# One hybrid decoder layer: another queue for the modulation rows, a later place for two kinds of stores

## The chip, the cores and the metric

The kernel runs on one core of a Trainium2 chip. The metric is the device time of one execution in microseconds (us). The engines are TensorE (PE), VectorE (DVE), ScalarE (ACT), GpSimd (POOL) and SyncE (SP). Each works through its own instructions in order. A transfer between HBM and the core's memory is issued by one of these engines as an instruction of its own; in the kernel before nearly all are issued by SP.

## What is computed

One layer for a sequence of 2048 tokens of width 1024, in float32:

```python
mod = jax.nn.silu(c) @ w_ada + b_ada                       # 6 * 1024 modulation values
shift1, scale1, gate1, shift2, scale2, gate2 = split(mod, 6)
h = rmsnorm(x, norm1_w) * (1 + scale1) + shift1
proj = h @ w_in                                            # q, k, v, z, xbc, dt
attn = sliding_window_attention(rope(q), rope(k), v, sinks)  # window 128
xbc = silu(causal_depthwise_conv(xbc, conv_w, conv_b))     # 1024 channels, width 4
y = ssd_chunked_scan(...) * silu(z), normalised by group   # Mamba-2, 8 heads, state 128
x = x + gate1 * (concat(attn, y) @ w_out)
h = rmsnorm(x, norm2_w) * (1 + scale2) + shift2
x = x + gate2 * ((silu(h @ w_g) * (h @ w_u)) @ w_down)     # width 2816
return rmsnorm(x, final_norm_w)
```

## The kernel before

Tokens are worked on in four blocks of 512. Every matrix product is made of three passes over halves: an operand is split into a high part (a rounded copy, made by ACT) and a low part (the difference, made by DVE or POOL), and `mm3` multiplies high by high, high by low and low by high.

**Weights.** `weight` (L259) makes one weight tile. The first block to use it loads the raw weight (L266, tile `raw`, 5 buffers), splits it (ACT L267, POOL or DVE L268, tile `w`, 6 buffers) and stores the two halves to HBM (L271); later blocks load the halves (L263). The stores are 16 of `wx` in block 0's `convolved`, 8 of `wz` in block 0's `gated`, 8 of `wq` and 4 of `wkv` in block 1, and 16 of `wo` in block 0's `out_proj`. That is 52 stores, of 512 KB (`wkv` 528 KB) each.

**Conv.** `convolved` (L467) makes the 8 tiles of 128 channels of a block with two weights each, runs the width-4 convolution over ACT, DVE and POOL, and stores each result tile `sx` (2 buffers) to `xs` in HBM (L490), 32 stores in all. The SSD part reads `xs` back by L682 in chunks of 128 tokens.

**Modulation.** The opening makes shift1 and scale1. The 32 other columns that are needed (gate1, scale2, shift2, gate2) are made by `ada_later` (L183), one column of 128 values per call: two loads of 256 KB each (L188, tile `aw`, 2 buffers), and a reduction on DVE for each (L194). The second reduction adds to the first. `tc.issue_after(last_fetched.ins)` ahead of the loads ties those that are issued by the engine of `last_fetched`, which is SP, to a place behind that instruction; the reductions are tied behind `first_done` on DVE in the same way. `rest_of_ada` calls `ada_later` for all 32 columns. It is attached to the main loop in block 2, but its loads start at 42.5 us.

**Order.** PE's order is that of the text (`manual_schedule`). In the opening the order of DVE, SP and ACT is that of the text too, among the instructions of the opening. Everywhere else a planner sets the order of each engine: it plays the program through with estimated times and issues, on each engine, what is ready, the earlier in the text first. The main loop goes through queries, keys and values, conv and gate of each block; `tick` (L1257) runs pieces of attention, SSD and other side work between the weights. Norms ahead of a block load x twice (L332), make the squares (L281, L284), and then the operands `hl` (DVE L324, ACT L326, DVE L327).

After the mixing part come the feed-forward products (`quad` and `down`, L949 and following), which the change does not touch.

Of the kernel before, what the change touches and what calls it, by code (L numbers as in the profile page):

```python
# [11 lines left out]
F32 = mybir.dt.float32  # L12
# [30 lines left out]
def hymba_layer(ctx, tc, xT, crow, pos, wada, wadk, vecs, rows, wq, wkv, wz, wx, wo, wgu, wd4, wd2, outT):  # L43
    nc = tc.nc
# [10 lines left out]
    def big(tag, bufs, dt=F32, pool=sb):  # L55
        return pool.tile([P, T], dt, name=tag, tag=tag, bufs=bufs)
# [8 lines left out]
    def dense():  # L65
        return bank("d", 4)
# [30 lines left out]
    def small(shape, name, bufs=2, dt=F32, pool=sb):  # L97
        return pool.tile(shape, dt, name=name, tag=name, bufs=bufs)
# [84 lines left out]
    def ada_later(i):  # L183
        halves = [slice(0, T), slice(T, D)]
        ws = [big("aw", 2, pool=ip) for _ in halves]
        with tc.issue_after(last_fetched.ins):
            for w, hs in zip(ws, halves):
                nc.sync.dma_start(w, wada[i, :, hs])  # L188
        for _ in range(2):
            yield  # L190
        m, pt = mod[:, i:i + 1], small([P, 1], "part", 2, pool=ip)
        with tc.issue_after(first_done.ins):
            for w, hs, src, dst in zip(ws, halves, (b_ada[:, i:i + 1], pt), (pt, m)):
                nc.vector.tensor_tensor_reduce(w, w, csil[:, hs], 0.5, src, ALU.mult, ALU.add, dst)  # L194
        yield
# [60 lines left out]

    split_d = {}

    def weight(src, n, key, store, eng=nc.gpsimd):  # L259
        two = wt.tile([P, 2, 528], F32R, name="w", tag="w", bufs=SPLIT)  # L260
        hi, lo = two[:, 0, :n], two[:, 1, :n]
        if key in split_d:
            nc.sync.dma_start(two[:, :, :n].bitcast(F32), split_d[key])  # L263
            return hi, lo
        raw = wt.tile([P, 528], F32, name="raw", tag="raw", bufs=RAW)
        nc.sync.dma_start(raw[:, :n], src)  # L266
        nc.scalar.activation(hi, raw[:, :n], AF.Copy)  # L267
        eng.tensor_tensor(lo, raw[:, :n], hi.bitcast(F32), ALU.subtract)  # L268
        if store:
            split_d[key] = dr.tile([P, 2, n], F32, name="w_" + "_".join(str(k) for k in key))  # L270
            nc.sync.dma_start(split_d[key], two[:, :, :n].bitcast(F32))  # L271
        return hi, lo

    def mm3(out, ahi, alo, bhi, blo, first, last):
        nc.tensor.matmul(out, ahi, bhi, start=first, stop=False)  # L275
        nc.tensor.matmul(out, ahi, blo, start=False, stop=False)  # L276
        mm3.last = nc.tensor.matmul(out, alo, bhi, start=False, stop=last)  # L277
# [85 lines left out]
    xs_d = [dr.tile([8, P, T], F32, name=f"xs{b}") for b in range(NB)]  # L363
# [18 lines left out]
    def tokens(b, h, name, srcs, n, toks, bank_of=lambda i: dense()):  # L382
        per = 2 if n == 256 else 1
        banks = [bank_of(i) for i in range(len(toks) // per)]
        plan = [(i, t, banks[i // per][:, i % per * n:i % per * n + n]) for i, t in enumerate(toks)]
        for kp in range(KT // 2):
            whi, wlo = weight(srcs[kp], 2 * n, (name, kp), b == (0 if name[0] == "z" else 1) and toks[-1] == NT - 1)
            for e in range(2):
                k, cs = 2 * kp + e, slice(e * n, (e + 1) * n)
                for i, t, out in plan:  # L390
                    ts = slice(t * P, (t + 1) * P)
                    mm3(out, h[k][0][:, ts], h[k][1][:, ts], whi[:, cs], wlo[:, cs],
                        k == 0 and i % per == 0, k == KT - 1 and i % per == per - 1)
            if kp < KT // 2 - 1 and (per == 2 or kp % 2):
                yield
        return [(t, out) for _, t, out in plan]
# [70 lines left out]
    def convolved(b, h):  # L467
        for c in range(8):
            ps = dense()
            for half in range(2):  # L470
                if half:
                    yield
                whi, wlo = weight(wx[c, half], T, ("x", c, half), b == 0, nc.gpsimd if half else nc.vector)
                for i in range(4):
                    k = 4 * half + i
                    ws = slice(i * P, (i + 1) * P)
                    mm3(ps, whi[:, ws], wlo[:, ws], h[k][0], h[k][1], k == 0, k == KT - 1)
            cin = small([P, T + 3], "cin", 2, pool=ip)
            nc.gpsimd.tensor_copy(cin[:, 0:3], halo[:, c, :])
            nc.scalar.copy(cin[:, 3:T + 3], ps)  # L480
            nc.gpsimd.tensor_copy(halo[:, c, :], cin[:, T:T + 3])
            cv, th, o = big("s", 3, pool=fw), big("s", 3, pool=fw), big("sx", 2, pool=ip)
            nc.scalar.activation(cv, cin[:, 0:T], AF.Identity, scale=conv_w[:, c, 0:1], bias=conv_b[:, c:c + 1])
            nc.scalar.activation(th, cin[:, 1:1 + T], AF.Copy, scale=conv_w[:, c, 1:2])
            nc.vector.scalar_tensor_tensor(cv, ps, conv_w[:, c, 3:4], cv, ALU.mult, ALU.add)
            nc.vector.scalar_tensor_tensor(th, cin[:, 2:2 + T], conv_w[:, c, 2:3], th, ALU.mult, ALU.add)
            nc.gpsimd.tensor_tensor(cv, cv, th, ALU.add)
            nc.scalar.activation(th, cv, AF.Tanh)
            nc.vector.scalar_tensor_tensor(o, th, 1.0, cv, ALU.add, ALU.mult)
            nc.sync.dma_start(xs_d[b][c], o)  # L490
            yield

    def gated(b, h):
        def gate(part, t, ps):
            z, th = staged(), big("s", 3, pool=fw)[:, 0:256]
            nc.scalar.activation(th, ps, AF.Tanh, scale=0.5)
            nc.vector.scalar_tensor_tensor(z, th, 1.0, ps, ALU.add, ALU.mult)
            nc.sync.dma_start(z_d[b * NT + t][:, part * 256:part * 256 + 256], z)
        yield from two_parts(b, h, "z", wz, gate)
# [746 lines left out]
    def rest_of_ada():  # L1246
        for i in (*range(16, 24), *range(32, 40), *range(24, 32), *range(40, 48)):
            yield from ada_later(i)
            if i == 39:
                nc.vector.scalar_tensor_tensor(scl2, mod[:, 32:40], 1.0, n2w, ALU.add, ALU.mult)  # L1250
            if i == 31:
                nc.vector.tensor_tensor(dsh, sh2[:, 4:8], sh2[:, 0:4], ALU.subtract)
        nc.vector.tensor_scalar(gate2, gate2, 0.5, None, ALU.mult)
# [56 lines left out]
    with tc.manual_schedule(engines={mybir.EngineType.PE}):  # L1310
# [8 lines left out]
        att = attentions(0, common)  # L1319
        sides.append(att)  # L1320
        run(convolved(0, h), 0.5)
        run(gated(0, h), 0.5)
        sides[:] = [both(att, ssds(0, stepping[0], extra))]
# [4 lines left out]
        run(keys_values(1, h), MIX)  # L1328
        prepared(1)
        run(convolved(1, h), MIX)  # L1330
        run(gated(1, h), MIX)
        mix1 = both(attentions(1, common), ssds(1, stepping[1], extra))
# [5 lines left out]
        prepared(2)  # L1338
        nxt = norm_ahead(3, (10, 15, 22))
        run(convolved(2, h), MIX)  # L1340
        finish(mix0)
        mix = []
# [163 lines left out]
def build(nc, arrays):  # L1506
    args = [nc.dram_tensor(f"in_{n}_dram", v.shape, mybir.dt.from_np(v.dtype), kind="ExternalInput").ap()
            for n, v in arrays.items()]
    out = nc.dram_tensor("out_0_dram", (NB, KT, P, T), F32, kind="ExternalOutput").ap()
    with tile.TileContext(nc, schedule_with_timeline_sim=True) as tc:  # L1510
        hymba_layer(tc, *args, out)
# [12 lines left out]
```

## Time and profile before

| | us |
|---|---|
| time, median of 3 runs | 2349.11 (2348.67 to 2351.01) |
| the profiled execution's own time | 2349.34 |
| its span, first to last instruction | 2347.3 |
| PE busy | 2239.9 |
| DVE busy | 1474.2 |
| POOL busy | 1216.1 |
| ACT busy | 969.8 |
| loads of modulation rows, first to last | 42.5 to 346.2 |
| stores of split weights, first to last | 70.0 to 546.1 |
| stores of conv results, first to last | 95.8 to 739.1 |

The span is 2.0 us shorter than the execution's own time. In the profile a row names line, engine, operation and the tiles written and read (`out<-in`); `SPq` and `ACTq` are the sequencers, which issue transfers and wait. A row of a wait names who waited, `<-` for whom, the total, how many times and the longest.

### The profile page before, as it was taken

To read this page: it belongs to the slowest core of one execution; us is meant where nothing else is said; L and a number is where in the kernel's file an instruction comes from. 1 tells how busy PE (TensorE), PEld (TensorE's weight loads), DVE (VectorE), ACT (ScalarE), POOL (GpSimd) and SP (SyncE) were. 2 spreads that over 40 slices of the span, in tenths; PEclk is the share of its full clock that TensorE was granted. 3 is DMA by queue.
4 is the path that set the end of the run, shared out by engine and by line. 5 is a ranking of instruction groups with operands and counts; after the bars stand their busy time and mean duration, and the time that the engine had idled before them with its cause. 6 is when DMAs were issued, how large, how long until landed. Compare 5 with 4: busy or idle time off the path is not lost. (4 is left out here: it accounts for less than half of the span.)

```text
span 2347.3 us, 33320 instructions
## 1 busy us (share of the span) xinstructions
PE 2239.9 (95%) x11292; PEld 1855.1 (79%) x11292; DVE 1474.2 (63%) x2629; ACT 969.8 (41%) x2020; POOL 1216.1 (52%) x1203
## 2 busy tenths in 40 slices
PE   6878989999999999999999999999999999999998
PEld 5778778888878788887877888767788888888787
DVE  8987975773578855666664353498645454454544
ACT  4564533654356645333333232344333333333332
POOL 2556433553223755687784332448666666653441
PEclk9989999999999999999999999999999999999999
DMA  8898887777888422332235765564422222273451
GB/s 299 296 322 305 301 252 251 252 245 254 291 271 310 141 72 81 101 99 88 95 102 164 256 217 177 185 222 144 144 81 81 81 81 81 81 227 102 142 172 63
DMA packets 252522, 418.52 MB, mean 178 GB/s; under 512 B 22848, under 2 KB 68928, under 8 KB 252352
## 3 DMA queue, kind: packets, MB, share of 16 engines
q1 hardware_dynamic: 251776, 415.87, 53.8%
q8 instruction: 89, 1.46, 0.3%
q14 instruction: 81, 0.66, 0.1%
q10 hardware_dynamic: 576, 0.52, 0.1%
HBM read 317.68 MB, written 98.63 MB: 177 GB/s over the span
## 5 line engine op out<-in xcount | busy, mean ns | idle before, releaser
L849 ACT ACTIVATE w<-raw 128x512 fp32r<-128x512 f32 x308 | 193.8, 630 | 428.5 <-PE d L277 225.1
L951 PE MATMUL d<-b,w 128*128 128x512 f32 x924 | 367.3, 399 | 1.3 <-POOL w L850 1.3
L949 PE MATMUL d<-b,w 128*128 128x512 f32 x924 | 365.1, 399 | 2.0 <-ACT t L980 1.3
L950 PE MATMUL d<-b,w 128*128 128x512 f32 x924 | 366.7, 397 | 0.3 <-POOL b L880 0.3
L275 PE MATMUL d<-a,w 128*128 128x512 f32 (+1 forms) x720 | 282.4, 396 | 10.2 <-DVE x L1060 5.2
L276 PE MATMUL d<-a,w 128*128 128x512 f32 (+1 forms) x720 | 282.2, 392 | 5.4 <-DVE a L844 5.3
L277 PE MATMUL d<-a,w 128*128 128x512 f32 (+1 forms) x720 | 283.9, 394 | 0.0
L850 DVE TENSOR_TENSOR w<-raw,w 128x512 fp32r<-128x512 f32 x220 | 209.0, 951 | 58.5 <-ACT w L849 57.7
L1060 DVE SCALAR_TENSOR_TENSOR x<-d,mod,x 128x512 f32<-128x512 f32 (+1 forms) x182 | 131.2, 724 | 173.9 <-PE d L277 171.9
L850 POOL TENSOR_TENSOR w<-raw,w 128x512 fp32r<-128x512 f32 x88 | 121.3, 1379 | 227.2 <-ACT w L849 209.9
L949 PEld LDWEIGHTS d<-b,w 128*128 128x128 f32 x924 | 174.3, 189 | 42.4 <-ACT t L980 2.5
L951 PEld LDWEIGHTS d<-b,w 128*128 128x128 f32 x924 | 174.0, 188 | 41.7 <-POOL w L850 1.5
L950 PEld LDWEIGHTS d<-b,w 128*128 128x128 f32 x924 | 174.6, 189 | 39.5 <-POOL b L880 0.7
L849 ACT ACTIVATE w<-s 128x512 fp32r<-128x512 f32 x176 | 111.1, 633 | 223.2 <-PE d L951 163.0
L850 POOL TENSOR_TENSOR w<-s,w 128x512 fp32r<-128x512 f32 x132 | 186.7, 1417 | 31.1 <-ACT w L849 30.3
L275 PE MATMUL d<-w,hl 128*128 128x256 f32 (+1 forms) x592 | 176.6, 298 | 7.7 <-ACT hl L326 5.0
L277 PE MATMUL d<-w,hl 128*128 128x256 f32 (+1 forms) x592 | 172.4, 291 | 2.2 <-DVE hl L327 2.2
L275 PEld LDWEIGHTS d<-a,w 128*128 128x128 f32 x720 | 136.3, 190 | 45.8 <-ACT a L1024 7.1
L276 PE MATMUL d<-w,hl 128*128 128x256 f32 (+1 forms) x592 | 172.1, 291 | 0.0
L276 PEld LDWEIGHTS d<-a,w 128*128 128x128 f32 x720 | 137.1, 190 | 38.3 <-DVE a L844 7.3
L277 PEld LDWEIGHTS d<-a,w 128*128 128x128 f32 x720 | 136.7, 190 | 30.4 <-issue 0.5
L965 POOL TENSOR_TENSOR s<-raw,s 128x512 f32<-128x512 f32 x44 | 58.6, 1332 | 186.7 <-DVE w L850 109.0
(393 smaller groups left out, 5437.7 us busy)
## 6 DMA issues: line engine op xcount, KB each, us to landing
raw<-in_wgu_dram SPq DMA_DIRECT2D x176, 256.0 KB, 2.7
raw<-in_wd_dram SPq DMA_DIRECT2D x176, 256.0 KB, 2.7
w<-w_x SPq DMA_DIRECT2D x48, 512.0 KB, 5.2
w<-w_o SPq DMA_DIRECT2D x48, 512.0 KB, 4.6
act<-t SPq DMA_DIRECT2D x88, 256.0 KB, 2.1
t<-act SPq DMA_DIRECT2D x88, 256.0 KB, 4.3
t<-in_xT_dram SPq DMA_DIRECT2D x80, 256.0 KB, 4.3
aw<-in_wada_dram SPq DMA_DIRECT2D x64, 256.0 KB, 4.5
```

Of the source, the lines that this page charges most:

```text
L275: nc.tensor.matmul(out, ahi, bhi, start=first, stop=False)
L276: nc.tensor.matmul(out, ahi, blo, start=False, stop=False)
L277: mm3.last = nc.tensor.matmul(out, alo, bhi, start=False, stop=last)
L849: nc.scalar.activation(hi, x, AF.Copy)
L850: eng.tensor_tensor(lo, x, hi.bitcast(F32), ALU.subtract)
L949: nc.tensor.matmul(out, ahi, bhi, start=first and k == 0, stop=False, skip_group_check=True)
L950: nc.tensor.matmul(out, ahi, blo, start=False, stop=False, skip_group_check=True)
L951: mm3.last = nc.tensor.matmul(out, alo, bhi, start=False, stop=k == 3, skip_group_check=True)
L965: nc.gpsimd.tensor_tensor(s4, a12, s2, ALU.subtract)
L1060: nc.vector.scalar_tensor_tensor(x, ps, gate2[:, c:c + 1], x, ALU.mult, ALU.add)
```

## The change

The loads in `ada_later` are issued by ACT in place of SP. The stores of split weights and of conv results are no longer issued where they stood: they are put on a list `owed` with a count of 2. Each call of `weight` first calls `settle`, which lowers the counts and issues on SP what has come to 0. At the end of `convolved` all that is still owed is issued. All bytes, tiles and buffer counts stay the same.

```diff
@@ ada_later
         with tc.issue_after(last_fetched.ins):
             for w, hs in zip(ws, halves):
-                nc.sync.dma_start(w, wada[i, :, hs])
+                nc.scalar.dma_start(w, wada[i, :, hs])
@@
+    owed = []
+
+    def settle():
+        for entry in list(owed):
+            entry[0] -= 1
+            if entry[0] == 0:
+                owed.remove(entry)
+                nc.sync.dma_start(*entry[1:])
+
     def weight(src, n, key, store, eng=nc.gpsimd):
+        settle()
...
-            nc.sync.dma_start(split_d[key], two[:, :, :n].bitcast(F32))
+            owed.append([2, split_d[key], two[:, :, :n].bitcast(F32)])
@@ convolved
-            nc.sync.dma_start(xs_d[b][c], o)
-            yield
+            owed.append([2, xs_d[b][c], o])
+            yield
+        for entry in list(owed):
+            owed.remove(entry)
+            nc.sync.dma_start(*entry[1:])
```

## The prediction

> **What bounds the kernel now.** I read the page first, then the busy times by stage, then who waits for whom in the stages that the change touches, then the queues' own order. The page says that TensorE (PE) is the bound almost everywhere.
>
> ```profile
> span 2347.3 us, 33320 instructions
> PE 2239.9 (95%) x11292; PEld 1855.1 (79%) x11292; DVE 1474.2 (63%) x2629; ACT 969.8 (41%) x2020; POOL 1216.1 (52%) x1203
> ```
>
> All of the idle time of PE is 2347.3 - 2239.9 = 107 us. The busy times by stage (columns: PE, its weight loads, DVE, ACT and POOL busy us with counts, then granted PE clock, DMA share, GB/s) show that the stretch from 60 to 352 us, where the modulation rows are loaded, holds 40 us of it, with a clock below 1 and DMA engines near full.
>
> ```profile
> 20.00:60.00 40.00, 39.79 (x266) 31.51 (x267) 37.51 (x57) 16.30 (x26) 12.31 (x9) 1.00 0.82 287
> 60.00:200.00 140.00, 116.89 (x685) 101.11 (x683) 118.24 (x277) 76.91 (x171) 69.53 (x68) 0.90 0.90 311
> 200.00:352.00 152.00, 134.72 (x876) 119.03 (x876) 128.76 (x321) 75.26 (x183) 78.69 (x117) 0.98 0.85 281
> ```
>
> That is (140.0 - 116.9) + (152.0 - 134.7) = 40.4 us, and it bounds from above what any mending of this stretch can give. DVE is busy for 85% of it, ACT for 52%. The waits of PE between 60 and 352 us (total, times, longest) say who ended the idle time.
>
> ```profile
> PE d L275 <- ACT hl L326: 5.0, 3, 2.3
> PE st L714 <- ACT m L793: 4.2, 1, 4.2
> PE am L275 <- ACT hl L326: 3.5, 1, 3.5
> PE at L589 <- DVE rsq L247: 3.3, 1, 3.3
> PE am L628 <- ACT m L592: 3.0, 1, 3.0
> PE d L277 <- DVE hl L327: 2.2, 4, 1.3
> PE d L275 <- ACT w L267: 2.1, 1, 2.1
> PE d L275 <- ACT bc L353: 2.0, 1, 2.0
> ```
>
> Two things are to be seen. No row says that PE waited for a weight's transfer; and ACT ended 8 of these waits, 5.0 + 4.2 + 3.5 + 3.0 + 2.1 + 2.0 = 19.8 us. So an ACT that runs later is felt by PE at once, while SP, which only issues transfers, acts on PE through others.
>
> **Part 1: the 64 loads of modulation rows go from SP to ACT.** Their rows in the kernel before:
>
> ```profile
> L188 SPq DMA_DIRECT2D aw<-in_wada_dram x64: 327/333/1177, 42.5 to 346.2; - x64
>   DVE aw L194: 22.8, 11
> SPq L188 <- DVE mod L194: 21.6, 14, 4.0
> SPq L188 <- DVE part L194: 19.1, 14, 2.7
> ```
>
> SP spends 64 x 0.333 = 21.3 us issuing them and 21.6 + 19.1 = 40.7 us held at them until DVE has reduced the rows that lay in the buffer before. DVE in turn stood 22.8 us, in 11 stalls, because a row had not landed. The worst place is around 180 us:
>
> ```profile
> 170.53 0.08 DVE L194 DVE_READ_ACCUMULATOR2_ANT mod<- 128x1 f32 x1
> 175.25 1.06 SPq L188 DMA_DIRECT2D aw<-in_wada_dram  x1
> 181.29 0.38 SPq L188 DMA_DIRECT2D aw<-in_wada_dram  x1
> 180.15 0.75 DVE L194 CUSTOM_DVE_ANT_0 aw<-aw,csil,part 128x512 f32<-128x512 f32 x1 [2.56 <-DMA aw<-in_wada_dram]
> 185.29 0.75 DVE L194 CUSTOM_DVE_ANT_0 aw<-aw,csil,vec 128x512 f32<-128x512 f32 x1 [4.37 <-DMA aw<-in_wada_dram]
> 176.87 0.39 PE L275 MATMUL d<-w,hl 128*128 128x256 f32 x1 [2.27 <-ACT hl L326]
> ```
>
> DVE freed a buffer at 170.6, SP came to its load at 175.25, and DVE then stood 2.56 and 4.37 us. The operands hl of block 1 are made by the same DVE, so the hl waits of PE behind this place are its price: of 5.0 + 2.2 = 7.2 us, 2.27 lie ahead of it at 176.87, which leaves 4.9 us. With the loads off SP this gap can shrink to nothing (-4.9) or not at all (0), as DMA is full here and the loads still need their time; between these I take half, **-2.5 us**.
>
> The other place where SP's order is felt is the wait at L589, 3.3 us: the transposes start as the load of q lands, which SP issued at 116.85 behind three of the modulation loads.
>
> ```profile
> 100.99 0.41 SPq L188 DMA_DIRECT2D aw<-in_wada_dram  x1
> 101.98 0.38 SPq L188 DMA_DIRECT2D aw<-in_wada_dram  x1
> 107.21 0.60 SPq L266 DMA_DIRECT2D raw<-in_wx_dram  x1
> 109.51 0.60 SPq L266 DMA_DIRECT2D raw<-in_wz_dram  x1
> 111.62 0.80 SPq L266 DMA_DIRECT2D raw<-in_wz_dram  x1
> 112.51 1.15 SPq L188 DMA_DIRECT2D aw<-in_wada_dram  x1
> 114.32 0.65 SPq L266 DMA_DIRECT2D raw<-in_wz_dram  x1
> 116.85 1.25 SPq L572 DMA_DIRECT2D m<-q  x1
> 118.15 0.71 SPq L266 DMA_DIRECT2D raw<-in_wz_dram  x1
> 119.45 0.52 SPq L271 DMA_DIRECT2D w_x<-w  x1
> ```
>
> Their issues are 0.41 + 0.38 + 1.15 = 1.94 us; bounds 0 and -3.3, I take **-1.9 us**.
>
> What ACT pays: the only transfers that ACT issues before are the last stores, at 0.338 us.
>
> ```profile
> L1081 ACTq DMA_DIRECT2D out_dram<-t x4: 338/338/377, 2341.9 to 2344.2; - x4
> SPq L1141 <- DMA csil<-in_crow_dram: 0.5, 1, 0.5
> L849 ACT ACTIVATE w<-raw 128x512 fp32r<-128x512 f32 x308 | 193.8, 630 | 428.5 <-PE d L277 225.1
> ```
>
> An issue on ACT waits in ACT's order, and behind it everything else of ACT: the splits of weights (L267), the operands (L326), the exponentials. If ACT comes to the buffer wait as early as SP does, one load costs it 0.338 + 40.7/64 = 0.97 us, 62 us in all; as ACT is idle for half of the stretch, most is covered, and PE sees only what falls into the ACT work just ahead of one of the 8 waits above. 64 loads in 304 us are one per 4.8 us; that work is about two ACT instructions of 0.63 us (row L849 below, the usual form), so 1.26 / 4.8 = 0.26 loads hit each of the 8: 8 x 0.26 x 0.97 = **+2.0 us**. The cover gone, all 8 hit, it is 8 x 0.97 = +7.8; the lower bound is 0. There is a second wait. The last x load of the opening waited for the landing of csil, which it does not use; csil is the transfer eight places before it. So a transfer is issued only when the one eight places earlier, on whichever queue, has landed; on ACT this becomes a wait of ACT. It is the rival below.
>
> The first two of the 64 have no earlier user of their buffers. On SP they are held behind the opening's last weight fetch, and start at 42.5; that hold orders only what SP itself issues, so on ACT nothing holds them. That the planner then moves such work to the front is shown by ACT's own order:
>
> ```profile
> 4.23 0.21 ACT L1242 ACTIVATE neg_a<-row 128x8 f32<-128x8 f32 x1 [1.41 <-DMA row<-in_rows_dram]
> 7.37 2.32 SPq L1158 DMA_DIRECT2D m<-in_wada_dram  x4
> ```
>
> L1242 is written after the whole opening, and yet runs at 4.23 us. Four issues in 2.32 us, each held for a landing, are one landing per (2.32 - 0.33)/3 = 0.66 us, for 256 KB. Two loads more ahead of x delay the first norm by 2 x 0.66 = 1.3 us, and behind it PE has 0.2 us and DVE 2.5 us of idle time between 20 and 60 us (first row of the stages), too little to make it up: **+1.3 us**, with bounds 0 (they stay behind) and +2.6 (the larger loads behind are held too).
>
> A rule of the Trainium skill speaks against this part: "DMA: Bandwidth & Descriptors", section "Issuing engines are not separate DMA queues", says that transfers from different engines share the same DMA engines, and that a second issuer saves issue time alone. By it neither -2.5 nor the rival's larger gain would be had, only issue time such as the 1.9 us, and the sum would be 2.5 us higher.
>
> **Part 2: stores two weights later.** 52 stores of split weights and 32 of conv results are written later in the text. I cost this at **0**, since SP's order comes from when a transfer is ready in the planner's reckoning, not from the text alone. The rows above show it: the last raw load of wx is issued at 107.21, the store of that weight at 119.45, and between them already four raw loads of wz. So SP is four weights ahead of the store, more than the two by which the text now moves it. A store is ready when its low half is; that does not change, and the raw load that becomes ready at the same moment is still written later than the store. A tile is released no later, as the store stays where it is; what is still owed when the conv of a block ends is issued there, ahead of its readers. The bounds come from the waits at these stores and at PE for weights:
>
> ```profile
> SPq L271 <- POOL w L268: 11.4, 7, 3.2
> PE am L276 <- POOL w L268: 1.0, 1, 1.0
> ```
>
> If the stores did move, 11.4 us of SP's holds would go, and PE could win the 2.1 + 1.0 us it waits for split weights and the rest of the 3.3 at q, 1.4: -4.5 us. If they held a weight tile longer, a split would start one store (0.5 us) later at two or three weights: +1.5.
>
> **The sum.** -2.5 - 1.9 + 2.0 + 1.3 + 0 = -1.1 us. The profiled execution took 2349.3 us (the 2347.3 of its span and 2.0 around it), 0.2 over the median of 2349.11. So 2348.2 in its terms and **2348.0** against the median. A difference of 0.2% (4.7 us) is about what a measurement of this kernel can tell from none; this is none.
>
> **The rivals.**
> *A, the rows come early and all stalls go.* On their own queue the loads do not stand behind SP's stores, land sooner, and DVE's 22.8 us of stalls go. For it: SP came 4.6 us late at 175.25. Against it: most of the 64 loads are held by DVE, not by SP's lateness (28 holds, 40.7 us), and DMA is at 0.85 to 0.90. Price: the 4.9 and 3.3 us whole, and the 3.5 us of the other hl wait, whose operand is made by a DVE that reduces rows in between: -11.7, with ACT's cost covered and the opening's +1.3 some -10, so 2339. "DMA: Bandwidth & Descriptors", section "Queues, rings and completion order", says that each DMA engine takes turns between the queues that have work; this is the mechanism by which a row would pass SP's backlog. No row of before has two busy queues, so none shows it.
> *B, ACT is held at SP's pace.* The wait for the transfer eight places earlier now stops ACT. At 170.6 the buffer is free, but the transfers ahead of that load were not all issued until 175.25; ACT would stand there for up to 4 us, again at 181.29, and likewise wherever SP is late. It decides from the point at which SP is later than DVE by more than ACT's slack ahead of an operand (the 2.27 at 176.87 shows that there is none). Price: two stalls of 4 us, the 7.8 us of the uncovered issue waits, half of the 4.9 lost again instead of won, and 1.3: 8 + 7.8 + 2.5 + 1.3 = +19.6 at most; not all places hit, I take half, +10, 2359.
> *C, the stores do move,* and the text's order wins: -4.5 on top of the sum's -1.1: 2349.1 - 5.6 = 2343.5.
>
> **How the numbers follow.** My forecast, no change that can be told, 0.33; A 0.27; C 0.12; B 0.28. A and C end faster, B slower. The likeliest one's own range is 2344.4 to 2353.8, 4.7 us to either side of the median. The range that reaches to the others: down to 2334 (A with the 2.1 and 2.0 us of weights and spread, and 1 of clock), up to 2364 (B nearly whole). Faster 0.39, same 0.33, slower 0.28.
>
> **What would show it.** The profile after should list 64 loads aw on ACT's queue, the first two before 5 us, with PE's first matmul 1.3 us later than now. SP's holds at L188 vanish; ACT shows holds for DVE L194. DVE's stalls at aw fall from 22.8 to some 15. Stores at L271 keep their places: the last of wx still behind about four raw loads of wz, with POOL's holds near 11.4 us up to 352 us. PE idle time from 60 to 352 us stays within 4 us of 40.4. If that falls under 32, A or C is right; if ACT's holds at the loads exceed 40 us and the waits of PE on ACT grow past 28, B. A first load that starts after 40 us takes away the +1.3.

## The result, and the profile after

The changed kernel takes 2359.73 us in the median of 4 runs (2358.64 to 2362.94), the kernel before 2349.2 us in its runs beside it. The medians differ by 10.5 us; the ratio of the two, worked out run against run, is 1.0035 with a 95% interval of 1.0023 to 1.0047. The change makes the kernel slower. The profiled execution is the 2362.94 us one, so its trace is 3.2 us longer than the median. Here and below, single executions that were disturbed (7730 us once in e1; 2478 and 9179 us once each in the kernel before) are left out of the ratios, though not of the medians.

The page of the profile after, first lines of the span and of the busy times:

```profile
span 2360.9 us, 33309 instructions
PE 2244.8 (95%) x11292; PEld 1858.5 (79%) x11292; DVE 1468.4 (62%) x2629; ACT 970.0 (41%) x2020; POOL 1218.3 (52%) x1203
```

Each engine has as many instructions as before: 11292 matmuls, 2020 of ACT. PE's idle time is 2360.9 - 2244.8 = 116.1 us, 8.7 more than before, and its busy time is 4.9 more, at a lower granted clock (0.979 in the mean of the execution, 0.983 before). PE's order is the text's, so the n-th matmul is the same one in every run here. Number 1830, which starts at 351.74 us in the kernel before, therefore marks the same amount of work everywhere. The busy times up to it and behind it, first of the kernel before, then of the changed one (columns as in the prediction; the first window ends where that matmul starts):

```profile
0.00:351.74 351.74, 292.98 (x1829) 253.16 (x1830) 296.47 (x687) 176.95 (x393) 165.07 (x241) 0.95 0.87 296
351.74:2347.30 1995.56, 1946.90 (x9465) 1601.97 (x9463) 1177.72 (x1943) 792.83 (x1628) 1051.08 (x962) 0.99 0.48 158
```

```profile
0.00:362.06 362.06, 297.16 (x1829) 257.09 (x1830) 297.26 (x690) 178.16 (x395) 167.38 (x241) 0.93 0.85 288
362.06:2360.90 1998.84, 1947.68 (x9465) 1601.41 (x9463) 1171.14 (x1939) 791.82 (x1626) 1050.94 (x962) 0.99 0.49 157
```

The stretch in which the rows are loaded takes 362.06 - 351.74 = 10.3 us longer. The rest differs by 3.3 us, as much as this execution lies over its median; among runs below that are no slower than the kernel before it takes from 1997.1 us (f2) to 2000.0 us (e5). So the loss that can be told is in the stretch. Of its 10.3 us, (362.06 - 297.16) - (351.74 - 292.98) = 6.1 are more idle time of PE and 297.16 - 292.98 = 4.2 are longer busy time for the same 1829 matmuls, at a granted clock of 0.93 in place of 0.95. Whether that clock is a part of the cause was not tested; f2 below has 0.94 in the stretch and no loss. The stretch moves the same bytes (351.74 us x 296 GB/s = 104.1 MB, 362.06 x 288 = 104.3 MB), with the DMA engines at 0.85 in place of 0.87.

The group of the 64 loads on ACT, with who waited for them (lines have moved: L277 is the split on ACT, L278 the low half, L266 the owed stores, L273 the load of stored halves, L276 the raw load, L336 the operand on ACT):

```profile
L188 ACTq DMA_DIRECT2D aw<-in_wada_dram x64: 334/334/452, 0.8 to 350.1; - x64
  DVE aw L194: 16.2, 12
```

The longest waits of SP from 60 to 352 us:

```profile
SPq L273 <- PE d L287: 25.4, 9, 5.4
SPq L276 <- POOL w L278: 24.8, 7, 5.6
SPq L266 <- POOL w L278: 23.4, 13, 4.4
```

DVE stands less for rows (16.2 us, 22.8 before). SP no longer waits for DVE at L188, but it is no freer: it now waits 24.8 + 23.4 us at raw loads and stores for the low halves of weights. The same two waits of the kernel before between 60 and 352 us:

```profile
SPq L271 <- POOL w L268: 11.4, 7, 3.2
SPq L266 <- POOL w L268: 6.1, 5, 1.6
```

POOL makes those halves from what ACT splits, and now ACT stands at the loads. From its timeline (start, duration, engine, line, operation; in brackets the idle time before it and what ended that):

```profile
81.74 0.57 ACT L490 COPY cin<-d 128x512 f32<-128x512 f32 x1
87.65 0.34 ACTq L188 DMA_DIRECT2D aw<-in_wada_dram  x1
88.09 0.81 ACT L493 ACTIVATE s<-cin,vec 128x512 f32<-128x512 f32 x1 [5.78 <-DMA raw<-in_wx_dram]
...
89.72 0.63 ACT L277 ACTIVATE w<-raw 128x512 fp32r<-128x512 f32 x1
94.59 0.34 ACTq L188 DMA_DIRECT2D aw<-in_wada_dram  x1
94.96 0.58 ACT L490 COPY cin<-d 128x512 f32<-128x512 f32 x1 [4.61 <-DMA raw<-in_wx_dram]
...
181.19 0.35 ACT L689 COPY m<-am 128x256 f32<-128x256 f32 x1
183.97 0.33 ACTq L188 DMA_DIRECT2D aw<-in_wada_dram  x1
184.35 0.72 ACT L336 ACTIVATE hl<-t,mod 128x512 fp32r<-128x512 f32 x1 [2.81 <-DMA w_q<-w]
```

The conv (L493) doesn't read a raw weight, and the operand (L336) doesn't read the store of a weight of q. ACT stood at the load ahead of them, and the landing that ended it is that of an earlier transfer on the same one of the eight semaphores that all transfers share in turn (175 or 176 of the transfers each). Adding up the idle time ahead of the 64 issues in the trace gives about 59 us: 26 until such a landing, and 32 more until DVE had freed the buffer. SP's own waits for landings, added up in the same way from 60 to 352 us, grow as well, from 9.5 to 27.8 us. PE behind these places (same columns):

```profile
90.41 0.50 PE L285 MATMUL d<-hl,w 128*128 128x512 f32 x1 [2.96 <-ACT w L277]
98.57 0.50 PE L285 MATMUL d<-hl,w 128*128 128x512 f32 x1 [2.66 <-ACT w L277]
185.12 0.58 PE L285 MATMUL d<-w,hl 128*128 128x256 f32 x1 [5.85 <-ACT hl L336]
191.38 0.58 PE L285 MATMUL d<-w,hl 128*128 128x256 f32 x1 [2.97 <-ACT hl L336]
```

What the trace does not say is whether these holds make the loss, or something else that came with the change: the stores, the two early rows, the planner's new order of the engines. The runs ask that.

### The profile page after: what moved, and what is told of

Its sections match the earlier page's. It is cut to its first block, busy times and chain, and to the rows that moved or that the text cites. A ratio compares the mean times of both kernels' runs of the same rounds, so it can differ in the third digit from the quotient of the medians.

```text
span 2360.9 us, 33309 instructions
## 1 busy us (share of the span) xinstructions
PE 2244.8 (95%) x11292; PEld 1858.5 (79%) x11292; DVE 1468.4 (62%) x2629; ACT 970.0 (41%) x2020; POOL 1218.3 (52%) x1203
## 3 DMA queue, kind: packets, MB, share of 16 engines
q1 hardware_dynamic: 242560, 399.09, 51.6%
## 5 line engine op out<-in xcount | busy, mean ns | idle before, releaser
L285 PE MATMUL d<-a,w 128*128 128x512 f32 (+1 forms) x720 | 282.1, 396 | 11.4 <-DVE x L1073 6.1
```

## The experiments

Each run was timed beside the kernel before on its own chip. Ratios are to that kernel, with 95% intervals; the chips differ by a few us, so times from different chips are compared by ratio. In the code cuts `...` stands for lines left out, and the comments are added for the reader.

| run | what it is | us | before, us | ratio |
|---|---|---|---|---|
| e1 | rows on ACT, stores as before | 2362.31 | 2352.78 | 1.0038 (1.0026 to 1.0050) |
| e2 | stores later, rows on SP | 2353.29 | 2352.78 | 1.0004 (0.9993 to 1.0015) |
| e3 | the change, first rows not before 50 us | 2365.56 | 2352.78 | 1.0053 (1.0039 to 1.0066) |
| f1 | rows on ACT, all else in the old order | 2363.95 | 2352.49 | 1.0051 (1.0038 to 1.0064) |
| f2 | rows on SP, all else in the order of e1 | 2351.21 | 2352.49 | 0.9998 (0.9988 to 1.0008) |
| e5 | ACT has the buffer's wait, planner's order | 2352.24 | 2352.97 | 0.9992 (0.9984 to 1.0001) |
| f3 | the same, old order | 2363.29 | 2352.49 | 1.0052 (1.0038 to 1.0065) |
| g1 | the same, order and places of e1 | 2365.06 | 2351.02 | 1.0056 (1.0044 to 1.0069) |
| e8 | 32 small stores on ACT | 2358.83 | 2352.97 | 1.0022 (1.0013 to 1.0032) |
| g2 | 64 small stores on ACT, order and places of e1 | 2364.86 | 2351.02 | 1.0063 (1.0049 to 1.0078) |
| g3 | 64 short ACT instructions without a wait | 2352.88 | 2351.02 | 1.0001 (0.9989 to 1.0013) |
| e4 | rows late, on SP | 2342.30 | 2352.78 | 0.9954 (0.9942 to 0.9967) |
| e9 | rows late, on ACT | 2344.15 | 2352.97 | 0.9957 (0.9942 to 0.9973) |
| e10 | rows late, on SP, reductions tied | 2332.43 | 2352.97 | 0.9913 (0.9900 to 0.9926) |
| e11 | rows late, on ACT, reductions tied | 2336.69 | 2352.49 | 0.9939 (0.9925 to 0.9953) |

### Which part of the change (e1, e2, e3)

e1 is the one line of the loads, on the kernel before:

```diff
-                nc.sync.dma_start(w, wada[i, :, hs])
+                nc.scalar.dma_start(w, wada[i, :, hs])
```

> The kernel before with the 64 row loads on ACT's queue; stores issued as before. Theory 1 (rival B, ACT is stopped at the loads and the opening's two early rows come ahead of x): all of the +10.6 us of the change is here, so 2359 us (2356 to 2362), two loads before 2 us, ACT held at L188 for some 30 us by DVE and 25 us by landings, as in the changed kernel. Theory 2 (the stores' later place in the text changes the planned order and costs it): 2347 to 2351 us. Half and half would be 2352 to 2355.

e2 is the rest of the change, `owed` and `settle`, with the loads left on SP.

> The kernel before with the stores written two weights later; row loads on SP's queue. Theory 1: no change, 2349 us (2347 to 2351), each store still about four raw loads behind its weight's raw load. Theory 2: 2355 to 2360 us. If the stores do move and help (rival C of the prediction) 2343 to 2346 us.

e3 is the change, with the loads tied behind an instruction of ACT:

```diff
-        with tc.issue_after(last_fetched.ins):
+        with tc.issue_after(last_split.ins):      # the opening's last split of a weight, on ACT
```

> The changed kernel, but the row loads on ACT are tied behind the opening's last split of a weight on ACT, so that the first two start near 50 us and not at 1 us. It takes away the opening's delay alone (PE's first matmul 1.55 us later, 2.5 us later by 24 us). Theory 1 (the holds of ACT after 60 us make the rest): 2357 us (2355 to 2359), first matmul at 14.6 us again. Theory 3 (the early pair shifts all that follows and makes the whole loss): 2349 to 2351 us.

The loads make all of it: e1 is as slow as the change, and e2 is the kernel before. In e2 ACT, DVE and POOL also run the same instructions in the same order as before up to 365 us, 398, 696 and 243 of them, and so does SP with its transfers; by the two traces this holds to the end. The later text moves nothing.

e3 was missed by every theory. The first matmul is back where it was, and the time is no better:

```profile
14.32 1.84 PE L1218 MATMUL at<-ones,t 128*128 128x2 f32 x8 [14.32 <-DVE t L295]
```

In the changed kernel that matmul started at 16.12 us. The opening's 1.8 us are real, but they are not a part of the sum: matmul 1830 starts at 364.8 us in e3, later than in the changed kernel. The stretch behind the opening sets when it ends.

### Holds, or the planner's order (f1, f2)

When the loads move, the planner reorders the other work: some 66 of ACT's 398 instructions up to 365 us and some 210 to 250 of DVE's 696 stand elsewhere in e1, by how the two orders are laid side by side. The order can be imposed, by a chain of order-only edges between the instructions of an engine. f1 is e1 with everything else in the order of the kernel before; f2 is the kernel before with everything else in the order of e1. Both add this at the end of the build, with the planned order of the other kernel as a list:

```diff
         hymba_layer(tc, *args, out)
+        pin(tc)            # PLANNED: places in the text, engine by engine, without the 64 loads
...
+        for a, b in zip(chain, chain[1:]):
+            tc.add_manual_dep(traced[b], traced[a].name, dep, reason="issue_after")
```

> The kernel before with the 64 row loads on ACT (as in the run with rows only), but every other instruction of ACT, DVE, POOL and SP is kept in the order that it has in the kernel before; only the places of the loads in ACT's order are new. Theory H (ACT is held at the loads, by landings of transfers eight places earlier, and passes it on): 8 to 12 us over the kernel before, as with rows only. Theory O (the holds cost little; moving the loads makes the planner order the engines' other work differently, 66 of ACT's 398 instructions up to 365 us and 251 of DVE's 696, and that order is worse): 0 to 3 us over. Between 4 and 7: both.

> The other half of it: the loads stay on SP, and ACT, DVE, POOL and SP have their other instructions in the order of the run with rows only. Theory H: within 3 us of the kernel before. Theory O: 7 to 12 us over it.

Theory H on both sides. e1 and f2 have the same order of everything and differ in who issues the 64 loads; so do f1 and the kernel before. Both pairs differ by 0.4 to 0.5%. The imposed edges cost nothing themselves, by f2 here and g3 below. Up to matmul 1830 the windows of f1 and of f2 read:

```profile
0.00:363.16 363.16, 295.33 (x1829) 255.16 (x1830) 298.87 (x690) 177.83 (x395) 164.96 (x241) 0.94 0.83 287
```

```profile
0.00:349.92 349.92, 292.36 (x1829) 253.88 (x1830) 291.81 (x687) 177.17 (x390) 163.29 (x241) 0.94 0.87 297
```

Again the same bytes (104.2 and 103.9 MB), with the DMA engines at 0.83 and 0.87. f2 shows something else: with e1's order it is late on the way (matmul 1101 starts at 228.9 us, 221.3 before), and yet it is on time at 350 us. A delay of PE within the stretch can be made up there. The changed kernel, too, is later on the way (matmul 1101 at 237.5 us, 16.2 later than before) than at the end (10.3).

### Which wait (e5, f3, g1, e8, g2, g3)

ACT has two waits at a load, and 64 more instructions. In e5 the loads are on SP, and ACT writes a few columns of the buffer first, so it has the buffer's wait alone:

```diff
             for w, hs in zip(ws, halves):
+                nc.scalar.activation(w[:, 0:8], csil[:, 0:8], AF.Copy)
                 nc.sync.dma_start(w, wada[i, :, hs])
```

> The kernel before, row loads on SP; ahead of each of the 64 loads ACT writes 8 columns of the buffer (an activation of 128x8, about 0.2 us), so that ACT has the wait for DVE's reduction of the buffer's earlier row, as in the changed kernel, but issues no transfer. Theory 1a (the wait for the buffer on ACT, 32 to 40 us of holds, is the main price): 2357 to 2363 us, 7 to 11 us over before. Theory 1b (the wait for the landing of the transfer eight places earlier, 19 to 23 us of holds, is the main price): 2350 to 2354 us. Both in proportion to their holds: 2356 us.

e8 gives ACT the landing's wait alone:

```diff
+        k = i - 16
+        with tc.issue_after(weight.splits[k * 45 // 31].ins):     # an early split of a weight, on ACT
+            nc.scalar.dma_start(notes[k], csil[0:8, 0:T])
```

> The kernel before, row loads on SP; in addition ACT issues 32 small stores of 16 KB from csil, a tile that nobody writes any more, one behind every one or two splits of a weight between 52 and 220 us. They wait for no buffer, only for the transfer eight places earlier. Theory 1b: ACT held 15 to 30 us at them by landings, and 2355 to 2362 us. Theory 1a: 2351 to 2354 us.

By these two the buffer's wait was free and the landing's wait cost half. But the trace of e8 shows the stores going out from 51.6 to 486.0 us, not by 220, and ACT hardly held at them, 1.6 us at one of them, so its 0.22% is not the price of holds; with some 60 to 100 of ACT's 398 instructions elsewhere it had an order of its own. And e5 had an order of its own too. f3 is e5 with everything else in the order of the kernel before:

> The run with ACT's write of 8 columns ahead of each load on SP, with every other instruction in the order of the kernel before. In the planner's own order it took no longer than before, with 50 us of holds for DVE at these writes. If that was no luck of the order, and holds for the buffer are free: within 2 us of the kernel before. If a better order hid their price: 4 to 9 us over.

It is 0.52% slower: that the holds were free in e5 was the doing of its order or its places. The last three put an instruction at the places where ACT issued loads. g1 (in e1's order) has there the write of e5, g2 (in e1's order) a small store like that of e8, and g3 (in the old order, at the places of f1) a write to a tile that nobody else uses:

```diff
+                nc.scalar.activation(posi.bitcast(F32)[:, 0:8], csil[:, 0:8], AF.Copy)   # g3
```

> All engines in the order of the run with rows only (which took 9 us more than before with the loads on ACT, and no more than before with the same order and the loads on SP). The loads are on SP; at the places where ACT issued a load it now writes 8 columns of the buffer (all but the first two places), so that ACT waits for DVE to free the buffer, and for no landing. The buffer's wait is the price: 8 to 11 us over before. The landing's wait is the price: 0 to 3 us over. Between: both have a part.

> The same order; the loads are on SP, and at the places where ACT issued a load it issues a store of 16 KB from a tile that nobody writes any more (all but the first two places), so that ACT waits for the landing of the transfer eight places earlier, and for no buffer. The 64 more transfers also lengthen SP's queue of such waits. The landing's wait is the price: 8 to 12 us over before. The buffer's wait is the price: 0 to 4 us over.

> All engines in the order of the kernel before, loads on SP; at the places that the loads had on ACT in the run with the old order (which took 11.5 us more than before) ACT writes 8 columns of a tile that nobody else uses any more, 0.2 us each, and waits for nobody (all but the first two). Only the time of 64 more instructions on ACT: 0 to 2 us over before if waits are the price, 6 us and more if ACT's time itself is.

What ended ACT's idle time ahead of these writes, by group (us, times), in g1, and the group in g3, which has no such row:

```profile
L188 ACT ACTIVATE aw<-csil x64: 191/208/217, 8.4 to 355.7; 128x8 f32<-128x8 f32 x64
  DVE mod L195: 35.3, 17
  DVE part L195: 27.1, 17
```

```profile
L188 ACT ACTIVATE posi<-csil x64: 191/193/218, 8.3 to 346.6; 128x8 f32<-128x8 f32 x64
```

64 instructions without a wait cost nothing (g3). The buffer's wait alone, 62.4 us of holds in g1, costs 0.56%, as much as the change. In g1 SP's loads stand behind ACT's writes, but SP is held there about as long as at the loads of the kernel before (42.9 and 40.7 us). Small stores, with a landing's wait and no buffer, cost 0.63% in g2; these 64 transfers are also new ones in the turn of the eight semaphores, which SP waits for too. Added up in the trace, ACT stands only 15.7 us at them, and SP's waits for landings from 60 to 352 us are 22.7 us, 12.3 in f2. So g2 says that transfers on ACT cost that much without any buffer, and not that ACT's own wait is all of it, or even most. The two prices don't add up: 0.56 and 0.63% alone, 0.38% for both in e1. Each of these two runs alone loses as much as the loads do.

The sum of the holds is not what counts. e5 and f3 have the same:

```profile
  DVE mod L195: 27.8, 19
  DVE part L195: 21.8, 17
  DVE dt L457: 4.3, 1
```

```profile
  DVE mod L195: 25.4, 16
  DVE part L195: 24.5, 12
  DVE dt L457: 4.7, 1
```

The rows shown are 53.9 us in e5, at no loss, and 54.6 us in f3, at 0.52%. In e5 the planner placed the writes and ordered the rest around them. Which places make the difference was not found.

### When the rows are loaded (e4, e9, e10, e11)

The stretch moves 104 MB at 0.87 of the DMA engines, and 64 x 0.262 = 16.8 MB of that are rows that nobody reads before the output products, from 512.7 us on (L820). e4 ties each load behind the last transfer of a weight that is written before it in the text:

```diff
-        with tc.issue_after(last_fetched.ins):
+        with tc.issue_after(weight.last.ins):     # set at both loads of weight()
```

> The kernel before, row loads on SP, each tied behind the last transfer of a weight that is written before it, so that the loads of the later blocks' rows go out with the later blocks' weights and not all before 352 us. PE is idle for 40.4 us from 60 to 352 us in the kernel before, with the DMA engines at 0.85 to 0.90 and DVE at 85%. If the rows' traffic and DVE's work on them in that stretch make a good part of it: 2335 to 2344 us, idle time there 25 to 32 us. If the stretch is bound by its weights without the rows: 2347 to 2351 us. If the late rows stall the blocks that use them: above 2352 us.

e9 is the same with the loads on ACT, tied behind the last split of a weight.

> Row loads on ACT, stores as before, each load tied behind the last split of a weight on ACT that is written before it, so that the loads go out late, as in the run with late rows on SP (2342 us). If the price is ACT's holds wherever the loads lie: 2349 to 2356 us, 7 to 12 us over the late rows on SP, with PE waiting on ACT behind the loads. If the price needs the full queue of the stretch up to 352 us: 2341 to 2345 us.

In e4 the loads go out from 293.1 to 675.8 us. Up to matmul 1830:

```profile
0.00:319.22 319.22, 281.14 (x1829) 245.12 (x1830) 253.50 (x567) 177.04 (x395) 153.93 (x241) 0.98 0.81 278
319.22:2342.40 2023.18, 1954.03 (x9465) 1606.23 (x9463) 1219.92 (x2062) 793.09 (x1626) 1058.26 (x962) 0.98 0.50 163
```

32.5 us are won there, and 2023.18 - 1995.56 = 27.6 us given back behind it, of which DVE's stalls at rows that have not landed were the suspect:

```profile
DVE aw L194 <- DMA aw<-in_wada_dram: 43.6, 24, 5.5
```

On ACT (e9) late loads cost no more than on SP: 0.9957 and 0.9954. That suggests that the price of ACT's queue belongs to the full stretch, but the pair differs in more than the queue: e9's loads go out from 201.4 to 629.7 us, and its matmul 1830 starts at 328.5 us, 9.3 later than in e4, which it makes up behind. e10 is e4 with each reduction tied behind the latest of four frequent instructions of DVE:

```diff
-        with tc.issue_after(first_done.ins):
+        with tc.issue_after(weight.dve.ins):      # set at L378, L489, L593 and L666
```

> The kernel with late rows on SP; in addition DVE's reduction of each row is tied behind the latest of four frequent DVE lines written before it (rope, conv, q's low half, the gated product's low half), so that DVE doesn't stand at a row that has not landed (43.6 us in 24 stalls with late rows). If these stalls are what gives back 28 of the 32 us won by 345 us: 2334 to 2339 us. If the give-back is the rows' traffic and DVE's own 94 us of reductions, which must be done somewhere: 2341 to 2345 us. If the later reductions hold the next loads and the blocks that read the rows: above 2346 us.

e11 is e9 with the same tie.

> The run with late loads on ACT (8.8 us under before), with DVE's reductions tied as in the run that took 2332 us. If ACT's queue costs nothing where the loads go out late: 2330 to 2336 us. If it costs even there, once DVE's stalls at the rows are gone: 2338 to 2344 us.

The stalls fall to 9.9 us in e10, and it is faster than any of its ranges and the fastest kernel here: 0.87% under the kernel before (0.74 to 1.00%), some 20 us, where the prediction's largest gain (rival A) was 11.7. What e10 wins over e4 lies behind the stretch:

```profile
0.00:317.77 317.77, 282.86 (x1829) 246.66 (x1830) 249.99 (x563) 176.90 (x395) 153.27 (x241) 0.97 0.81 279
317.77:2329.80 2012.03, 1949.13 (x9465) 1606.70 (x9463) 1216.24 (x2066) 791.76 (x1626) 1057.60 (x962) 0.99 0.50 164
```

2023.18 - 2012.03 = 11.2 us. With the same tie, ACT's queue may show again: e11, between its two ranges, is 0.9939 to e10's 0.9913, and the intervals just touch.

## Why the prediction was wrong, step by step

**The step that failed is what ACT pays, +2.0.** It put a price of 0.97 us on each load, let ACT's idle half cover it except where one of PE's eight waits on ACT stood behind it, and put the sum without any cover at +7.8. Measured, with the loads in the full stretch, loads or writes that make ACT wait cost 9 to 13 us in four runs of five (e1 0.38%, f1 0.51%, f3 0.52%, g1 0.56%, and e5 nothing), more than the uncovered bound. Two things were wrong in it. The price of one load was too small: ACT paid (59 + 64 x 0.334) / 64 = 1.26 us, and up to 5.3 us of hold at one load (5.8 with its issue, the row of the conv above), since a landing's wait comes on top. The 40.7 us of SP's holds also left out two smaller rows of the same view:

```profile
SPq L188 <- DVE s L378: 4.5, 4, 2.0
SPq L188 <- DVE m L377: 4.3, 1, 4.3
```

At 1.26 us a load the same sum gives 2.6 us, so the larger error is the cover. It was judged at PE's waits on ACT alone, while a late ACT also goes on through others: it splits late, POOL makes the low half late, and SP stands at raw loads and stores for it, 48 us in the changed kernel against 17.5 before, so that later transfers are issued later. That this is the path of the loss is argued, not shown: in g1, where SP waits for ACT's writes instead, these two waits are no longer than before and the loss is as large.

```profile
SPq L272 <- POOL w L269: 9.7, 7, 3.9
SPq L267 <- POOL w L269: 4.9, 4, 1.6
```

The term failed, then, in what covers a hold of ACT; by which path PE loses the time stays open. Of the other terms 0.6 us came at q's load and no other gain or loss that can be told (below), so that by the measured 10.5 us this term is about 11, an estimate.

**Rival B had the size and the wait.** It named the wait for the transfer eight places earlier as a wait of ACT, with two stalls near 175.25 and 181.29 us, and gave 2359; the changed kernel has holds at 183.97 and at 189.23 us, as the same work comes there, and takes 2359.7. Its own working was less right than its number: its +10 is half of a largest sum of +19.6, so that the 2359 is in part luck, and it counted landings' holds and operands, while the buffer's wait alone does as much (g1). It had 0.28 of the chance, against 0.33 for no change. Its mark at ACT came true, holds over 40 us (59); its mark at PE did not: the waits of PE on ACT were to grow past 28 us. The waits of PE from 60 to 365 us in the changed kernel:

```profile
PE d L285 <- ACT hl L336: 8.8, 2, 5.9
PE d L285 <- DVE s L388: 6.9, 2, 5.8
PE d L285 <- ACT w L277: 5.6, 2, 3.0
PE st L754 <- DVE m L743: 3.3, 1, 3.3
PE at L641 <- DVE m L606: 3.3, 2, 3.0
PE am L641 <- ACT m L605: 2.9, 1, 2.9
PE at L602 <- DMA m<-q: 2.7, 1, 2.7
```

The rows of ACT add up to 17.3 us here, 19.8 in the prediction; with the rows that are too small to be shown it is 19.8 here and 20.4 before (60 to 352 us). So the loss did not reach PE as waits on ACT.

**The idle time between fixed times could not tell.** Between 60 and 352 us PE is idle for (140.0 - 111.7) + (152.0 - 138.7) = 41.6 us in the changed kernel, 40.4 before, and by the prediction that spoke for no change. But the same work now needs 10 us more, and what no longer fits in the window is not counted as idle:

```profile
60.00:200.00 140.00, 111.68 (x617) 95.88 (x616) 110.85 (x267) 74.80 (x165) 67.95 (x66) 0.86 0.88 300
200.00:352.00 152.00, 138.69 (x920) 123.75 (x918) 131.43 (x316) 75.04 (x178) 80.27 (x111) 0.97 0.85 280
```

1537 matmuls in the place of 1561.

**-2.5 for the gap behind 180 us** did not come. DVE's stalls fell as said, from 22.8 to 16.2 us (about 15 was foretold), but the operands were late at the same place for ACT's sake, 5.85 and 2.97 us of PE. Rival A falls with it. The Trainium skill ("DMA: Bandwidth & Descriptors", section "Issuing engines are not separate DMA queues") says that a second issuer saves issue time alone. The trace doesn't go against that: 64 x 0.333 = 21.3 us of issues left SP, and the kernel gained nothing by it.

**-1.9 for q's load** came in part: PE waits 2.7 us for it now (row above), 3.3 before.

**+1.3 for the early rows** was right as a local time, 16.12 - 14.56 = 1.56 us at the first matmul with the loads issued at 0.80 and 1.25 us, and wrong as a term: without it (e3) the kernel is no faster.

**0 for the stores** held: e2 is 1.0004 (0.9993 to 1.0015), and up to 365 us the orders are the same. That POOL's holds of SP at the stores would stay near 11.4 us was wrong, for ACT's sake and not for the stores': they are 23.4 us in the changed kernel, and 25.9 in e1, where the stores stand as before.

## What to carry to other kernels

Before a transfer is moved to an engine that computes, list all its waits, for the buffer and for the semaphores that it shares with other queues, and ask what stands behind each in that engine's order: SP stood 40 us at these loads at no price that was found, and ACT, in four runs of five, could not. Compare a stretch that is fed by transfers from one matmul to the same matmul, never between fixed times, and don't add up local gaps of PE in it. And look first at what need not be in the full stretch at all: loading 16.8 MB later won 0.46%, and 0.87% with the reductions tied as well, where moving the loads to another queue lost 0.35%.

## What was not expected

Equal holds of ACT, 54 us in e5 and in f3, cost nothing in one order of the other work and 0.52% in another; this is open. The writes with the buffer's wait (0.56%) and the small stores with the landing's (0.63%) cost more alone than the loads with both waits (0.38%). And a PE that is 7.6 us late at matmul 1101 (f2) was on time 120 us later. A pace that something other than PE sets would explain the last two: the DMA engines are at 0.83 to 0.87 in the whole stretch, and e4, which takes 104.1 - 88.7 = 15.4 MB and DVE's reductions of them out of it, ends it 32.5 us earlier. Of these, 292.98 - 281.15 = 11.8 us are shorter busy time of PE for the same matmuls, at a granted clock of 0.98 in place of 0.95, and 20.7 less idle time. Whether the DMA engines, DVE or the clock set that pace was not told apart, as late rows change all three.
